# Weight buffers at three offsets within 128 bytes of SBUF, in a two-layer decoder kernel

## The chip, the cores and the metric

The kernel runs on one core of a Trainium2 chip. The metric is the device time of one execution in microseconds; each version is timed in several runs and the median is taken. A profile is one further execution with the hardware profiler on, which gives a start and a duration for every instruction.

The engines are TensorE (PE in the profile, with its weight loads shown apart as PEld), VectorE (DVE), ScalarE (ACT), GpSimd (POOL) and SyncE (SP), which here issues the DMAs. They run side by side and wait for one another through semaphores. SBUF is the on-chip memory with 128 partitions; a tile's address is an offset in bytes within each partition. PSUM takes the products of TensorE.

## What is computed

Two decoder layers on 256 tokens of width 2048. Layer 0 is a sliding-window attention with 32 query heads, 8 key and value heads and a learned sink per head; layer 1 is an RG-LRU recurrent block. Each is followed by a gated feed-forward block with a short causal convolution over positions. Cut to what matters here:

```python
def conv_ffn(h, w_up, conv_w, conv_b, w_down):
    u = causal_dwconv(h @ w_up, conv_w, conv_b)        # 2048 -> 2 x 6144, 3 taps
    g, v = jnp.split(u, 2, axis=-1)
    return (jax.nn.gelu(g, approximate=True) * v) @ w_down

for layer in range(2):
    h = rmsnorm(x, mix_norm[layer])
    x = x + (sliding_window_attention(h, ...) if layer == 0 else rglru_block(h, ...))
    x = x + conv_ffn(rmsnorm(x, ffn_norm[layer]), ...)
```

All inputs and the output are float32. The matrices hold some 100 million weights, each of which is read once.

## The kernel before

**Layout.** Activations stay in SBUF, transposed: features on partitions, the 256 tokens along the free axis. Weights come from HBM in chunks of 1 MiB, [128 partitions x 2048] float32, 376 of them in one fixed list (`order`): keys 4, values 4, queries 16, attention output 16, then the first feed-forward block with 96 up-projection and 48 down-projection chunks, recurrent input 32, recurrent output 16, and the second feed-forward block with 96 and 48 again. The gates of the recurrent block have 8 smaller loads of their own.

**Two parts of each weight.** A float32 weight `w` is split into `hi` and `lo`, two numbers in the shorter format float32r whose sum is `w`. Activations are split likewise. A product is hi*hi + hi*lo + lo*hi. With a block of 128 x 128 weights stationary, `hi` meets 512 columns, the activation's two parts side by side (`mm_hi`, line 183), and `lo` meets 256 columns, the activation's first part (`mm_lo`, line 189). A chunk holds 16 such blocks, so it makes 16 matmuls of 512 columns and then 16 of 256, each with its own weight load of 128 columns. In the down projections a chunk is used as two half batches of 8 and 8.

**The stream of chunks.** Each chunk passes three buffers: `raw` (written by a DMA that SyncE issues, line 102), `hi` (ACT casts `raw`, line 109) and `lo` (DVE subtracts `hi` from `raw`, line 117). Each of the three has its own pool with three buffers, which the chunks take in turn. `advance()` issues one DMA, one cast and one subtraction, for chunks ahead of the one in use; it is called after each chunk's matmuls. The order of instructions on every engine is the order in which the program is written.

**Moving operands.** The queries, keys, up projections (`pu`) and the recurrent input projection (`px`, `py`) stream `h`, which lies in the pool `per`. The attention's output projection (`po`) streams `ao`, the down projections (`pd`) `g`, the recurrent output projection (`pr`) `z`: these lie in pools that are opened after the weight pools, behind them in SBUF. In the value projection (`pv`) the roles are swapped: `h` is stationary and the weights stream.

**Where tiles lie.** A pool lays its tiles one behind another in the order in which they are first asked for; small tiles take at least 32 bytes. In `per` the tiles ahead of the weights have sizes of whole multiples of 128 bytes but for the last three, `sp`, `sp4` and `sp8`, of 64 bytes each. Every weight buffer has 8192 bytes, so all nine start at 64 modulo 128. `x` and `h` start at 0 modulo 128.

**Small attention tiles.** `kg` (two gains), `kq` (their product, one column), `snk` (the sinks) and `nsnk` (their negative), and `rc`, `rct`, `rcv` (two columns each, for the norm's factor along the partitions) are tiles of their own in the pool `attn`.

Of the kernel before, what the change touches and what calls it, by code (L numbers as in the profile page):

```python
"""Two decoder layers on one core: sliding-window attention with sinks + ConvFFN, then an RG-LRU
block + ConvFFN.

Activations stay on chip, transposed: features on partitions, the 256 tokens along the free
axis.  Weights stream through SBUF once, in 1 MiB chunks.  A float32 operand is split exactly into
two float32r parts (w = hi + lo, 12 significant bits each); a product is hi*hi + hi*lo + lo*hi,
accumulated in float32 in PSUM.  With the weight's part stationary, hi streams [x_hi | x_lo] and lo
streams x_hi, so a projection's PSUM bank holds hi*hi in its first half and the cross terms in its
second.

RMSNorm's per-token factor is applied to a projection's output, since it commutes with the product.
"""
# [7 lines left out]
F32 = mybir.dt.float32  # L20
F32R = mybir.dt.float32r
AF = mybir.ActivationFunctionType
ALU = mybir.AluOpType
# [17 lines left out]
def trunk(ctx, tc, xT, wq, wk, wv, wo, win, wg, wout, wup, wdn, mixg, ffng, kqg, sinks,  # L41
# [10 lines left out]
    hip = ctx.enter_context(tc.tile_pool(name="hip", bufs=3))  # L52
    lop = ctx.enter_context(tc.tile_pool(name="lop", bufs=3))
# [51 lines left out]
    def split_hi():  # L105
        c = st["hi"]
        if c < NCH:
            his[c] = hip.tile([P, CH], F32R, tag="hi", name=f"hi{c}")
            act.copy(out=his[c], in_=raws[c])  # L109
            st["hi"] += 1  # L110

    def split_lo(part=slice(0, CH)):
        c = st["lo"]
        if c < NCH:
            if part.start == 0:
                los[c] = lop.tile([P, CH], F32R, tag="lo", name=f"lo{c}")
            dve.tensor_tensor(out=los[c][:, part], in0=raws[c][:, part], in1=f(his[c][:, part]), op=ALU.subtract)  # L117
            if part.stop == CH:
                raws.pop(c)
                st["lo"] += 1  # L120
# [6 lines left out]
    def use():  # L127
        """The next chunk's parts."""
        c = st["use"]
        st["use"] += 1  # L130
        return his.pop(c), los.pop(c)
# [5 lines left out]
    def step(g):  # L137
        """Runs a generator to its next yield."""
        if g is not None:
            next(g, None)  # L140

# [1 line left out]
    def split_x(dst, src, gains, k):  # L143
        """dst[:, k] = the two parts of src * gain (src [P, T])."""
        act.activation(out=dst[:, k, 0, :], in_=src, func=AF.Copy, scale=gains[:, k:k + 1])
        dve.scalar_tensor_tensor(out=dst[:, k, 1, :], in0=src, scalar=gains[:, k:k + 1],
                                 in1=f(dst[:, k, 0, :]), op0=ALU.mult, op1=ALU.subtract)

    def stat(src, first):
        """sqa += src * src (src [P, 2, T])."""  # L150
        if first:
            pool.tensor_tensor(out=sqa, in0=src, in1=src, op=ALU.mult)
        else:
            pool.tensor_tensor(out=sqt, in0=src, in1=src, op=ALU.mult)  # L154
            pool.tensor_tensor(out=sqa, in0=sqa, in1=sqt, op=ALU.add)
# [5 lines left out]
    def rsqrt1(y, v):  # L161
        """A first guess of v ** -0.5."""
        act.activation(out=y, in_=v, func=AF.Ln)
        act.activation(out=y, in_=y, func=AF.Exp, scale=-0.5)

    def rsqrt2(y, v, tmp):
        """One Newton step towards v ** -0.5."""
        dve.tensor_tensor(out=tmp, in0=v, in1=y, op=ALU.mult)
        dve.scalar_tensor_tensor(out=tmp, in0=tmp, scalar=-0.5, in1=y, op0=ALU.mult, op1=ALU.mult)
        dve.scalar_tensor_tensor(out=y, in0=tmp, scalar=1.5, in1=y, op0=ALU.add, op1=ALU.mult)  # L170
# [21 lines left out]
    def x_epi(ps, d, n, gains, tp, out_=None, tag="xt"):  # L192
        """x's tiles d .. d + n take the product in ps [P, n, 512]; then h's, or the output's."""
        t = tp.tile([P, n, T], F32, tag=tag, name=f"xt{st['use']}")
        xs = x[:, d:d + n, :]
        for i in ([slice(0, n)] if out_ is None else [slice(i, i + 1) for i in range(n)]):
            dve.tensor_tensor(out=t[:, i], in0=ps[:, i, 0:T], in1=xs[:, i], op=ALU.add)  # L197
            dve.tensor_tensor(out=xs[:, i], in0=ps[:, i, T:], in1=t[:, i], op=ALU.add)  # L198
            if out_ is not None:
                nc.sync.dma_start(out=out_[:, d:d + n, :][:, i], in_=xs[:, i])  # L200
        if out_ is not None:
            return
        yield
        if gains is None:
            return
        for i in range(d, d + n):
            split_x(h, x[:, i, :], gains, i)
        yield
        if n == 2:
            stat(xs, d == 0)  # L210
        elif d % 2:
            stat(x[:, d - 1:d + 1, :], d == 1)

    def late_pair(ps, rhs, mid=None):
        """Two output tiles whose operand's last two k-tiles come late."""
        parts = [use(), use()]
        for i, (hi, lo) in enumerate(parts):
            mm_hi(ps[:, i], hi, rhs, rng(0, KD - 2))
            mm_lo(ps[:, i], lo, rhs, rng(0, KD - 2), stop=False)
        advance()  # L220
        if mid:
            mid()
        for i, (hi, lo) in enumerate(parts):
            mm_hi(ps[:, i], hi, rhs, rng(KD - 2, KD), start=False)
            mm_lo(ps[:, i], lo, rhs, rng(KD - 2, KD))
        advance()

    def softplus():
        """sp = softplus(-lam) = max(-lam, 0) + log1p(e), e = exp(-|lam|), by the series of
        log1p(e) = 2 artanh(z), z = e / (2 + e) <= 1/3."""  # L230
# [25 lines left out]
    for c in range(3):  # L256
        raws[c] = rawp.tile([P, CH], F32, tag="raw", name=f"raw{c}")
        his[c] = hip.tile([P, CH], F32R, tag="hi", name=f"hi{c}")
        los[c] = lop.tile([P, CH], F32R, tag="lo", name=f"lo{c}")
# [12 lines left out]
    # ================= attention =================  # L272
    with ExitStack() as ph:
# [10 lines left out]
        kq = ap_.tile([P, 1], F32, name="kq")  # L284
        kg = ap_.tile([P, 2], F32, name="kg")
        snk = ap_.tile([P, 32], F32, name="snk")
        nsnk = ap_.tile([P, 32], F32, name="nsnk")
        cb = ap_.tile([P, T], F32, name="cb")
        cc = ap_.tile([P, 2, 2], F32, name="cc")
        rc = ap_.tile([P, 2], F32, name="rc")  # L290
        rct = ap_.tile([P, 2], F32, name="rct")
        rcv = ap_.tile([P, 2], F32, name="rcv")
# [16 lines left out]
        # key j of two blocks is seen from query i when i < j <= i + 128  # L309
# [36 lines left out]
        dve.tensor_scalar(out=nsnk, in0=snk, scalar1=-1.0, scalar2=None, op0=ALU.mult)  # L346

# [13 lines left out]
        def k_fin(p):  # L361
# [11 lines left out]
            dve.scalar_tensor_tensor(out=s, in0=s, scalar=kq[:, 0:1], in1=r, op0=ALU.mult, op1=ALU.mult)  # L373
# [5 lines left out]
        def kv_norm():  # L379
            """The first norm's factor along the free axis and along the partitions."""  # L380
# [97 lines left out]
        def softmax(j, S):  # L478
            # column 2 * b + a: block b, head a
# [15 lines left out]
            ns = nsnk[:, 2 * j:2 * j + 2].unsqueeze(1).to_broadcast([P, 2, 2])  # L495
# [39 lines left out]
        def values(j):  # L535
# [3 lines left out]
            for b in range(2):  # L539
                # (key block, slice of the transposed probabilities)  # L540
# [15 lines left out]
        def attend(j, ps, hi, lo, rhs, nk):  # L556
            """One output tile's products over nk of its k-tiles; between them the steps of the
            attention of the query tiles j - 1 and j - 2."""
# [79 lines left out]
    # ================= ConvFFN =================  # L638
# [64 lines left out]
    # ================= RG-LRU =================  # L703
    with ExitStack() as ph:
# [6 lines left out]
        def projected(ps, n, eng):  # L711
            """A pair of output tiles: the two halves of the bank added, times the norm's factor."""
# [8 lines left out]
        with ExitStack() as px:  # L721
# [48 lines left out]
            def gates_rest(n, ps):  # L770
                """r (kept in a), i * x (in u), and t = tanh(4 sp r)."""
# [54 lines left out]
        # a = exp(-8 sp r) = 1 - t (1 + a), and sqrt(1 - a a) = sqrt(t) (1 + a)  # L826
# [37 lines left out]
        # (n, i): what follows the products of tile i of the y projection's pair n, before the stream  # L864
        # moves on and after it
# [58 lines left out]
def _layout(inp):  # L924
    import numpy as np

    def cols(w):
        """[K, N] -> [N / 128, 128, K / 128, 128]: chunk per 128 columns, rows on partitions."""
# [3 lines left out]
    def vec(v):  # L932
        """[..., n * 128] -> [128, ..., n]"""
# [49 lines left out]
```

## Time and profile before

| what | value |
|---|---|
| median of 3 runs | 2217.95 us (2217.54 to 2218.45) |
| span of the profiled execution | 2215.8 us |
| PE busy (matmuls) | 2185.9 us, 99% |
| PEld busy (weight loads) | 1921.5 us, 87% |
| DVE, ACT, POOL busy | 1568.6, 1142.7, 186.7 us |
| subtractions for `lo` (line 117) | 390 pieces, 858.1 us, 2200 ns each |
| casts for `hi` (line 109) | 373, 713.0 us, 1912 ns each |
| DMA | 405.15 MB, mean 183 GB/s |

The only execution time of the profiled run that the profile gives is its span, from the first to the last instruction; the median of the runs is 2.15 us above it. In the timeline view each row has a start, a duration, the engine, the line, the operation, the tile written and those read, shapes, and how many instructions are merged into it. A matmul's duration reaches past the start of the next one, since matmuls are pipelined; the rate is read from start to start.

### The profile page before, as it was taken

The page shows a single profiled execution, that of the slowest core. Times are in us where ns is not written, and L with a number is a line of the kernel's source. Part 1 is how long each engine was busy: PE and PEld are TensorE (multiplying, and loading weights), DVE is VectorE, ACT ScalarE, POOL GpSimd, SP SyncE. Part 2 cuts the span into 40 slices and gives each one's busy share as a digit, 9 for nine tenths or more (in the row PEclk, how much of TensorE's full clock was granted, in tenths as well). Part 3 has the DMA queues.
Part 4 walks back from the last instruction along what each step waited for, and adds up shares of the span by engine and source line. Part 5 has one row for each costly group of instructions (what it writes and reads, how often), then busy time and mean ns, then how long its engine had stood idle before and what let it go on. Part 6 is the DMA issues. An engine that isn't in the chain of part 4 may idle for free.

```text
span 2215.8 us, 30701 instructions
## 1 busy us (share of the span) xinstructions
PE 2185.9 (99%) x12656; PEld 1921.5 (87%) x12656; DVE 1568.6 (71%) x1862; ACT 1142.7 (52%) x1400; POOL 186.7 (8%) x155
## 2 busy tenths in 40 slices
PE   7999999999999999999999979999999999999999
PEld 6888888888888888888889868888888888888888
DVE  7877767777644777776677787777776457777654
ACT  4777445555433555553366744455554335555432
POOL 4122220000000000002200143200000000000000
PEclk9999999999999999999999999999999999999999
DMA  6333555555555555555465445555555555555543
GB/s 218 134 116 116 189 189 208 191 190 190 190 186 194 187 192 191 191 190 189 163 223 176 163 152 194 186 191 190 190 190 192 190 188 190 190 190 190 190 190 133
DMA packets 61053, 405.15 MB, mean 183 GB/s; under 512 B 7537, under 2 KB 9969, under 8 KB 13169
## 3 DMA queue, kind: packets, MB, share of 16 engines
q1 hardware_dynamic: 60912, 403.19, 51.3%
q8 instruction: 99, 1.62, 0.3%
q14 instruction: 42, 0.34, 0.0%
HBM read 401.06 MB, written 2.10 MB: 182 GB/s over the span
## 4 chain that ended last, share of the span: by engine, by line
PE 93%; DVE 3%; ACT 2%; issue 1%; POOL 1%; DMA 0%; SPq 0%; DVEq 0%; ACTq 0%
PE pu L183 32%; PE pu L189 16%; PE pd L183 16%; PE pd L189 8%; PE px L183 3%; PE po L183 3%; PE pr L183 3%; PE pq L183 2%; PE px L189 2%; PE pr L189 1%; PE po L189 1%; PE pq L189 1%; PE O L544 1%; DVE lo L117 1%; POOL ps L717 1%
## 5 line engine op out<-in xcount | busy, mean ns | idle before, releaser
L117 DVE TENSOR_TENSOR lo<-raw,hi 128x2048 fp32r<-128x2048 f32 (+1 forms) x390 | 858.1, 2200 | 223.8 <-ACT hi L109 222.6
L109 ACT CAST hi<-raw 128x2048 fp32r<-128x2048 f32 x373 | 713.0, 1912 | 386.1 <-PE pd L183 248.0
L183 PE MATMUL pu<-h,hi 128*128 128x512 f32 x3072 | 736.7, 392 | 0.0
L183 PEld LDWEIGHTS pu<-h,hi 128*128 128x128 f32 x3072 | 563.0, 188 | 111.2
L189 PEld LDWEIGHTS pu<-h,lo 128*128 128x128 f32 x3072 | 383.5, 188 | 16.4
L189 PE MATMUL pu<-h,lo 128*128 128x256 f32 x3072 | 387.0, 278 | 0.0
L183 PE MATMUL pd<-g,hi 128*128 128x512 f32 x1536 | 384.6, 392 | 0.0
L183 PEld LDWEIGHTS pd<-g,hi 128*128 128x128 f32 x1536 | 276.2, 189 | 49.4
L189 PEld LDWEIGHTS pd<-g,lo 128*128 128x128 f32 x1536 | 209.6, 190 | 14.9
L189 PE MATMUL pd<-g,lo 128*128 128x256 f32 x1536 | 214.2, 282 | 0.0
L666 ACT CAST g<-us 128x256 fp32r<-128x256 f32 x96 | 39.0, 406 | 280.7 <-DVE us L665 280.7
L659 DVE SCALAR_TENSOR_TENSOR uy<-us,fw,uy 128x255 f32<-128x255 f32 (+1 forms) x384 | 176.7, 481 | 6.8
L651 DVE TENSOR_TENSOR us<-pu,ua 128x512 f32<-128x512 f32 x96 | 66.4, 692 | 154.7 <-ACT ua L650 154.6
L650 ACT COPY ua<-pu 128x512 f32<-128x512 f32 x96 | 56.3, 587 | 143.4 <-PE pu L189 143.4
L656 ACT ACTIVATE uy<-us,fb,fw 128x256 f32<-128x256 f32 x192 | 104.8, 596 | 2.7 <-DVE us L652 2.7
L197 DVE TENSOR_TENSOR xt<-pd,x 128x512 f32<-128x512 f32 (+1 forms) x40 | 23.3, 583 | 83.3 <-PE pd L189 83.3
L154 POOL TENSOR_TENSOR sqt<-x 128x512 f32<-128x512 f32 x28 | 64.5, 2305 | 179.1 <-DVE x L198 176.6
L183 PE MATMUL px<-h,hi 128*128 128x512 f32 x320 | 77.7, 395 | 0.0
L667 DVE TENSOR_TENSOR g<-us,g 128x256 fp32r<-128x256 f32 x96 | 40.8, 425 | 45.3 <-ACT g L666 45.3
L183 PE MATMUL pr<-z,hi 128*128 128x512 f32 x256 | 63.1, 396 | 8.8 <-DVE z L861 7.8
L183 PE MATMUL pq<-h,hi 128*128 128x512 f32 x256 | 71.3, 403 | 0.2 <-DVE vh L442 0.2
L183 PEld LDWEIGHTS px<-h,hi 128*128 128x128 f32 x320 | 58.8, 189 | 11.8
(195 smaller groups left out, 1844.2 us busy)
## 6 DMA issues: line engine op xcount, KB each, us to landing
raw<-in_wup SPq DMA_DIRECT2D x192, 1024.0 KB, 4.8
raw<-in_wdn SPq DMA_DIRECT2D x96, 1024.0 KB, 4.8
raw<-in_win SPq DMA_DIRECT2D x32, 1024.0 KB, 4.8
raw<-in_wq SPq DMA_DIRECT2D x16, 1024.0 KB, 4.7
raw<-in_wo SPq DMA_DIRECT2D x16, 1024.0 KB, 4.8
raw<-in_wout SPq DMA_DIRECT2D x16, 1024.0 KB, 4.8
raw<-in_wv SPq DMA_DIRECT2D x4, 1024.0 KB, 5.4
graw<-in_wg SPq DMA_DIRECT2D x8, 512.0 KB, 3.4
```

The lines of the kernel that those rows point to most:

```text
L109: act.copy(out=his[c], in_=raws[c])
L117: dve.tensor_tensor(out=los[c][:, part], in0=raws[c][:, part], in1=f(his[c][:, part]), op=ALU.subtract)
L154: pool.tensor_tensor(out=sqt, in0=src, in1=src, op=ALU.mult)
L183: pe.matmul(ps, lhsT=hi[:, off + k * n:off + k * n + P], rhs=rhs[:, xk].rearrange("p a t -> p (a t)"), start=start and k == ks[0][0], stop ...
L189: pe.matmul(ps[:, T:], lhsT=lo[:, off + k * n:off + k * n + P], rhs=rhs[:, xk, 0, :], start=False, stop=stop and k == ks[-1][0])
L197: dve.tensor_tensor(out=t[:, i], in0=ps[:, i, 0:T], in1=xs[:, i], op=ALU.add)
L650: act.copy(out=a, in_=ps[:, :, 0:T])
L651: dve.tensor_tensor(out=s, in0=ps[:, :, T:], in1=a, op=ALU.add)
L656: act.activation(out=y[:, i, :], in_=s[:, i, :], func=AF.Identity, scale=fw[:, layer, n, 2:3], bias=fb[:, layer, n:n + 1])
L659: dve.scalar_tensor_tensor(out=y[:, i, tap:], in0=s[:, i, 0:T - tap], scalar=fw[:, layer, n, 2 - tap:3 - tap], in1=y[:, i, tap:], op0=ALU. ...
L666: act.copy(out=g[:, m, 0, :], in_=s[:, 0, :])
L667: dve.tensor_tensor(out=g[:, m, 1, :], in0=s[:, 0, :], in1=f(g[:, m, 0, :]), op=ALU.subtract)
```

## The change

The three `hi` buffers and the three `lo` buffers are no longer three buffers of one tag, but three tags of one buffer each, taken by the chunk's number modulo 3. Behind each is a pad of 64, 32 and 32 bytes that nobody uses, so that the three start at 64, 0 and 32 modulo 128. The pads of a pool sum to 128 bytes, so what follows starts at the same offset modulo 128 as before. `raw` stays as it was. Of the small attention tiles, `kq` becomes the first column of `kg`, `nsnk` is written over `snk`, and `rc`, `rct`, `rcv` become columns of one tile. Comments were removed, with line numbers kept.

```diff
-    hip = ctx.enter_context(tc.tile_pool(name="hip", bufs=3))
-    lop = ctx.enter_context(tc.tile_pool(name="lop", bufs=3))
+    hip = ctx.enter_context(tc.tile_pool(name="hip", bufs=1))
+    lop = ctx.enter_context(tc.tile_pool(name="lop", bufs=1))
...
+    def part_tile(c, pool_, what):
+
+        return pool_.tile([P, CH], F32R, tag=f"{what}{c % 3}", name=f"{what}{c}")
+
+    def pad(pool_, what, n):
+        pool_.tile([P, n // 4], F32, name=f"pad_{what}{n}_{len(pads)}")
+        pads.append(n)
+
+    pads = []
...
-            his[c] = hip.tile([P, CH], F32R, tag="hi", name=f"hi{c}")
+            his[c] = part_tile(c, hip, "hi")
             act.copy(out=his[c], in_=raws[c])
...
-                los[c] = lop.tile([P, CH], F32R, tag="lo", name=f"lo{c}")
+                los[c] = part_tile(c, lop, "lo")
...
     for c in range(3):
         raws[c] = rawp.tile([P, CH], F32, tag="raw", name=f"raw{c}")
-        his[c] = hip.tile([P, CH], F32R, tag="hi", name=f"hi{c}")
-        los[c] = lop.tile([P, CH], F32R, tag="lo", name=f"lo{c}")
+        his[c] = part_tile(c, hip, "hi")
+        pad(hip, "hi", (64, 32, 32)[c])
+        los[c] = part_tile(c, lop, "lo")
+        pad(lop, "lo", (64, 32, 32)[c])
...
-        kq = ap_.tile([P, 1], F32, name="kq")
         kg = ap_.tile([P, 2], F32, name="kg")
+        kq = kg[:, 0:1]
         snk = ap_.tile([P, 32], F32, name="snk")
-        nsnk = ap_.tile([P, 32], F32, name="nsnk")
...
-        rc = ap_.tile([P, 2], F32, name="rc")
-        rct = ap_.tile([P, 2], F32, name="rct")
-        rcv = ap_.tile([P, 2], F32, name="rcv")
+        rcs = ap_.tile([P, 3, 2], F32, name="rcs")
+        rc, rct, rcv = rcs[:, 0], rcs[:, 1], rcs[:, 2]
...
-        dve.tensor_scalar(out=nsnk, in0=snk, scalar1=-1.0, scalar2=None, op0=ALU.mult)
+        dve.tensor_scalar(out=snk, in0=snk, scalar1=-1.0, scalar2=None, op0=ALU.mult)
...
-            ns = nsnk[:, 2 * j:2 * j + 2].unsqueeze(1).to_broadcast([P, 2, 2])
+            ns = snk[:, 2 * j:2 * j + 2].unsqueeze(1).to_broadcast([P, 2, 2])
```

More of the change, by code (lines that the diff above doesn't have):

```diff
@@ L372, in k_fin @@
             rsqrt2(r, v, t)
-            dve.scalar_tensor_tensor(out=s, in0=s, scalar=kq[:, 0:1], in1=r, op0=ALU.mult, op1=ALU.mult)
+            dve.scalar_tensor_tensor(out=s, in0=s, scalar=kq, in1=r, op0=ALU.mult, op1=ALU.mult)
             for i in range(2):
```

## The prediction

> **What bounds the kernel now.** I read the page first, then stretches of single stages, then the order of TensorE's instructions in time.
>
> ```profile
> span 2215.8 us, 30701 instructions
> PE 2185.9 (99%) x12656; PEld 1921.5 (87%) x12656; DVE 1568.6 (71%) x1862; ACT 1142.7 (52%) x1400; POOL 186.7 (8%) x155
> PE 93%; DVE 3%; ACT 2%; issue 1%; POOL 1%; DMA 0%; SPq 0%; DVEq 0%; ACTq 0%
> ...
> L117 DVE TENSOR_TENSOR lo<-raw,hi 128x2048 fp32r<-128x2048 f32 (+1 forms) x390 | 858.1, 2200 | 223.8 <-ACT hi L109 222.6
> L109 ACT CAST hi<-raw 128x2048 fp32r<-128x2048 f32 x373 | 713.0, 1912 | 386.1 <-PE pd L183 248.0
> ```
>
> TensorE is never without work, and the chain that ended last is 93% TensorE. Two stretches, one of the up projection and one of the down projection (columns: length, then busy time and count for PE, PEld, DVE, ACT, POOL, then granted clock, DMA share, GB/s):
>
> ```profile
> 325.00:436.00 111.00, 111.00 (x646) 97.64 (x645) 87.50 (x105) 65.33 (x75) 0.00 (x0) 1.00 0.57 200
> 600.00:655.00 55.00, 55.00 (x318) 48.48 (x317) 26.71 (x16) 19.10 (x10) 0.00 (x0) 1.00 0.55 191
> ```
>
> No gap and a granted clock of 1.00. So the time is the number of matmuls times their pitch (start to start), and only a changed pitch moves the end. The pitch is not one number. In the order of time, TensorE's batches of `hi` (512 columns) and `lo` (256 columns), up projection, then output projection of the attention, then down projection:
>
> ```profile
> 325.16 3.84 PE L183 MATMUL pu<-h,hi 128*128 128x512 f32 x16
> 328.84 1.98 PE L189 MATMUL pu<-h,lo 128*128 128x256 f32 x16
> 330.65 3.82 PE L183 MATMUL pu<-h,hi 128*128 128x512 f32 x16
> 334.31 2.05 PE L189 MATMUL pu<-h,lo 128*128 128x256 f32 x16
> 336.20 1.09 PE L183 MATMUL pu<-h,hi 128*128 128x512 f32 x4
> ```
>
> ```profile
> 240.79 3.82 PE L183 MATMUL po<-ao,hi 128*128 128x512 f32 x16
> 244.44 2.08 PE L189 MATMUL po<-ao,lo 128*128 128x256 f32 x16
> 246.36 0.86 PE L183 MATMUL po<-ao,hi 128*128 128x512 f32 x3
> ...
> 600.36 1.12 PE L189 MATMUL pd<-g,lo 128*128 128x256 f32 x8
> 601.32 2.00 PE L183 MATMUL pd<-g,hi 128*128 128x512 f32 x8
> 603.16 1.11 PE L189 MATMUL pd<-g,lo 128*128 128x256 f32 x8
> 604.11 2.00 PE L183 MATMUL pd<-g,hi 128*128 128x512 f32 x8
> ```
>
> From start to start, `pu` takes 3.68 + 1.81 us for one chunk and 3.66 + 1.89 for the next, 11.04 for two: **5.52 us a chunk**, with two kinds of `lo` batch (113 and 118 ns a matmul). `po` takes 3.65 + 1.92: **5.57** (120 ns a `lo`). `pd` takes 0.96, 1.84, 0.95 for half batches: 2 x (1.84 + 0.955) = **5.59**. Shapes, engine and clock are the same; the moving operand differs. From the tile sizes in the code, `h` starts at 0 modulo 128 bytes, while `ao`, `g` and all nine weight buffers start at 64: `sp`, `sp4` and `sp8` are 64 bytes each and every other long-lived tile ahead of the weights is a multiple of 128. So weights less moving operand is 64 for `pu` and 0 for `po` and `pd`. `z` is at 64 too, and its row agrees (3.65 and 1.92). The attention's value product has weights `vh` at 64 against `pt` at 0 (behind the small attention tiles, which take 32 bytes or more each):
>
> ```profile
> 1334.41 3.82 PE L183 MATMUL pr<-z,hi 128*128 128x512 f32 x16
> 1338.06 2.08 PE L189 MATMUL pr<-z,lo 128*128 128x256 f32 x16
> 1339.98 0.40 PE L183 MATMUL pr<-z,hi 128*128 128x512 f32 x1
> ...
> 110.17 1.22 PE L544 MATMUL O<-pt,vh 128*128 128x256 f32 x9
> 111.22 0.63 PE L183 MATMUL pq<-h,hi 128*128 128x512 f32 x2
> ```
>
> 1.05 us for 9 is 117 ns: like `lo` at difference 64, not the 120 of difference 0. I take it that a matmul's stream and the weight load that runs under it (PEld, 87% busy) delay each other, by an amount that depends on this difference. A `hi` less a `lo` of `po` is (3.65 - 1.92) / 16 = 108 ns for 256 columns, so the columns alone would be 216 and 108 ns; the excess of 12 ns on both is what one weight load costs there.
>
> **The change, part by part.** The instructions stay: same casts, subtractions, matmuls, DMAs, in the same order. Three tags with one buffer each, chosen by chunk modulo 3, rotate as one tag with three did, so each cast waits for the same matmuls as now (the 248.0 us behind L109, off the chain). Merging `kq` into `kg`, `nsnk` into `snk`, and `rc`, `rct`, `rcv` into one tile joins operations that already follow one another; a wait between them would come once, before the query tiles, and is bounded by one microsecond. I put it at 0. What moves is the weights' start: 64, 0 or 32 for chunks 0, 1, 2 modulo 3, `hi` and `lo` alike. `g`, `ao`, `z` stay at 64, since the pads sum to 256 bytes.
>
> DVE and ACT now read and write `hi` and `lo` at other offsets than `raw` (64). If that slows them it is hidden: in the stretch 325 to 436, 20 chunks long, DVE is idle for 23.5 us and ACT for 45.7, so a subtraction may grow by 1.2 us on its 2.2 and a cast by 2.3 on its 1.9 before TensorE waits. Only beyond that would each further 0.1 us cost 192 x 0.1 = 19 us. Nothing in the rows suggests it.
>
> TensorE, by stage (chunks of 1 MiB: `pu` 192, `pd` 96, `po` and `pr` 32, `px` and `py` 32, attention 24):
>
> - *Chunks that go to a known difference.* A third of `pu` goes from 64 to 0: 64 x (5.57 - 5.52) = **+3.2 us**. A third of `pd` goes from 0 to 64. Taking halves of the `pu` batches, 2 x (1.835 + 0.925) = 5.52: 32 x (5.52 - 5.59) = **-2.2**. For `po` and `pr`, 10.7 x (5.52 - 5.57) = **-0.5**.
> - *`pu` chunks that stay at 64.* Half of their `lo` batches run at 1.81 today, and which kind comes depends on how the `hi` batch ahead ended. With neighbours at other differences the fast kind may be lost: 64 x 0.04 = +2.6 at worst, or come always: -2.6. I take half the loss, **+1.3**, as the slow kind is what follows any disturbance in `px`:
>
> ```profile
> 1137.97 3.90 PE L183 MATMUL px<-h,hi 128*128 128x512 f32 x16
> 1141.70 2.05 PE L189 MATMUL px<-h,lo 128*128 128x256 f32 x16
> 1143.59 3.83 PE L183 MATMUL px<-h,hi 128*128 128x512 f32 x16
> 1147.25 2.05 PE L189 MATMUL px<-h,lo 128*128 128x256 f32 x16
> 1149.14 0.29 PE L765 MATMUL g<-xc,ghi 128*128 128x256 f32 x1
> ```
>
> - *`px`, `py`.* 11.17 / 2 = 5.585 with the gates between, against 5.57 at difference 0: **0**; attention likewise (24 chunks, some 0.4 us either way).
> - *Chunks at difference 32 (`pu`) or -32 (`pd`, `po`, `pr`).* No row shows this. Bounds from the rows: the best batches seen, 3.65 + 1.81 = 5.46, and the worst, 3.73 + 1.92 = 5.65. I take the middle between the two known differences, 5.545, because 32 lies between them: 64 x 0.025 - 32 x 0.045 - 10.7 x 0.025 = 1.6 - 1.4 - 0.3 = **-0.1**. At the lower bound it is -3.8 - 4.2 - 1.2 - 1.3 = -10.5, at the upper +8.3 + 1.9 + 0.9 + 0.7 = +11.8 (the last term is `px` and `py`).
>
> Sum: 3.2 - 2.2 - 0.5 + 1.3 - 0.1 = +1.7 on the span of 2215.8, so 2217.5. The median of the runs is 2217.95, 2.15 above the span, which gives **2219.7 us**.
>
> A rule speaks against any effect. The Trainium skill (TensorE: Matmul & The Clock Gate, Step-by-step: what each phase is for) says that weight loads and the moving operand have separate read ports, so "Loading the next tile's weights doesn't steal SBUF read bandwidth from the running matmul." By it the sum would be 0 and the time 2218.0. The trace does not bear it out: 113, 118 and 120 ns for one shape at clock 1.00.
>
> **The rivals.**
>
> *Nothing depends on the offset* (the change doesn't do what it says): the differences between `pu` and `po` come from something else about `h`, its place below the weights for instance. Then 2218.0. Against it: `O`, both of whose operands lie above the weights, runs like `pu`; `pr`, `po` and `pd` agree with each other. For it: the two kinds of `lo` exist at one offset, so something besides the offset counts. By the rule just named this is the outcome.
>
> *Difference 32 keeps the two streams apart.* Then the best rows hold: 1.8 - 10.5 gives 2218.0 + 1.8 - 10.5 = 2209 (1.8 is the sum without the -0.1). Were the load fully hidden, a chunk would be 16 x 324 ns = 5.19 us: 64 x -0.33 - 32 x 0.40 - 21.4 x 0.39 = -42, or 2177. For it: the rates do vary with the offset. Against: no stage, with whatever tile, shows a stream without the excess.
>
> *Difference 32 is the worst of all* (the slower side). Place: the weight loads of buffer 2, some 118 chunks (64 + 32 + 10.7 + 10.7) of 32 loads, 3,776 loads. A load that starts in the middle of a 64-byte piece touches nine pieces of its 512 bytes where it touched eight, and meets the stream once more; and the loads of `h`'s stages lose the fast `lo`. At the worst rows: 1.8 + 11.8 = +13.6, or 2231.6. Each nanosecond a load is 3.8 us, so it decides, past 0.2%, from about 1 ns a load above the middle; were the 12 ns paid twice it would be +45, or 2263. For it: 64 and 0, the known cases, both start on a piece of 64 bytes, and nothing tells what lies between. Against: the excess is small against 108 ns in every row. The Trainium skill (SBUF — State Buffer, Door 1) gives lines of 16 bytes, by which 32 would be as good a start as 64; no run here shows the line's size.
>
> **How the numbers follow.** Forecast 0.40, no dependence 0.08, apart 0.22, worst 0.30: the slower side is above the faster because the known terms are already at +1.8. What can be told from no change is 0.2%, 4.4 us, so 2213.5 to 2222.4 is the same. Forecast and no dependence fall there but for 0.01 on each side: faster 0.23, same 0.46, slower 0.31. The range takes in both bounds, 2209 and 2231.6, and part of the tails beyond: 2203 to 2240. The forecast's own range is 2214 to 2225.
>
> **What would show it.** Every third `pu` chunk should show 3.65 + 1.92 like `po`, and every third `pd` half chunk should fall from 0.955 to 0.91 to 0.945 for `lo`; the chunk after, of buffer 2, gives the price of 32 directly. If `pu` chunks of all three buffers keep the present pattern, the offset is not the cause. If DVE or ACT slow beyond the slack above, gaps appear in PE with L117 or L109 as releaser. A gap-free PE whose batches leave 3.65 to 3.73 or 1.81 to 1.92 makes the prediction wrong in its largest unknown.

## The result: 1% slower

The changed kernel takes a median of 2241.32 us (2240.86 to 2241.78) against 2218.2 us before: a ratio of **1.0106, interval 1.0092 to 1.012**. The forecast was 2219.7 us. The page's first lines, after:

```profile
span 2239.1 us, 30701 instructions
PE 2209.9 (99%) x12656; PEld 1934.2 (86%) x12656; DVE 1571.0 (70%) x1862; ACT 1141.1 (51%) x1400; POOL 186.6 (8%) x155
...
L126 DVE TENSOR_TENSOR lo<-raw,hi 128x2048 fp32r<-128x2048 f32 (+1 forms) x390 | 857.9, 2200 | 225.4 <-ACT hi L118 223.8
L118 ACT CAST hi<-raw 128x2048 fp32r<-128x2048 f32 x373 | 711.2, 1907 | 395.2 <-PE pd L192 251.2
```

The number of instructions on each engine is the same. Subtractions still take 2200 ns and casts 1907 (1912 before), so the offsets did not slow the subtractions and casts. TensorE's busy time grew by 24 us, and the part of the span in which it is not busy stayed (29.9 us before, 29.2 after). In two stretches of single stages it has no gap (columns: length, then busy time and count for PE, PEld, DVE, ACT, POOL, then granted clock, DMA share, GB/s):

```profile
329.00:430.00 101.00, 101.00 (x577) 88.49 (x576) 78.28 (x94) 56.64 (x66) 0.00 (x0) 1.00 0.55 195
600.00:655.00 55.00, 55.00 (x317) 48.18 (x317) 26.40 (x16) 19.07 (x10) 0.00 (x0) 1.00 0.54 192
```

The clock is 1.00 as before. So the pitch changed. Three consecutive chunks of an up projection, then two half batches of `hi` and of `lo` of a down projection, in the order of time (starts in the first column):

```profile
348.68 3.89 PE L192 MATMUL pu<-h,hi 128*128 128x512 f32 x16
352.41 2.08 PE L198 MATMUL pu<-h,lo 128*128 128x256 f32 x16
354.33 3.90 PE L192 MATMUL pu<-h,hi 128*128 128x512 f32 x16
358.06 2.05 PE L198 MATMUL pu<-h,lo 128*128 128x256 f32 x16
359.95 3.82 PE L192 MATMUL pu<-h,hi 128*128 128x512 f32 x16
363.61 2.09 PE L198 MATMUL pu<-h,lo 128*128 128x256 f32 x16
365.53 0.40 PE L192 MATMUL pu<-h,hi 128*128 128x512 f32 x1
```

```profile
607.08 1.99 PE L192 MATMUL pd<-g,hi 128*128 128x512 f32 x8
608.90 1.13 PE L198 MATMUL pd<-g,lo 128*128 128x256 f32 x8
609.87 2.01 PE L192 MATMUL pd<-g,hi 128*128 128x512 f32 x8
611.71 1.12 PE L198 MATMUL pd<-g,lo 128*128 128x256 f32 x8
612.67 2.02 PE L192 MATMUL pd<-g,hi 128*128 128x512 f32 x8
```

The up projection's chunks of buffers 2, 0 and 1 take 3.73 + 1.92 = 5.65, 3.73 + 1.89 = 5.62 and 3.66 + 1.92 = 5.58 us, where before two took 11.04. The mean is 5.617, against 5.517 before: 192 x (5.617 - 5.517) = **+19 us of the 23**. A down-projection chunk shown takes 1.82 + 0.97 + 1.84 + 0.96 = 5.59; averaged over the matmuls' starts it is 5.605 against 5.587, so 96 chunks give +1.7. The rest is spread over the other 88 chunks. The surprise is buffer 0: its `hi` and its `lo` start at 64 modulo 128 as ever, and a chunk in them costs 0.10 us more.

### The profile page after: what moved, and what is told of

It reads as the page before. It is cut to its first block, busy times and chain, and to the rows that moved or that the text cites. A ratio compares the mean times of both kernels' runs of the same rounds, so it can differ in the third digit from the quotient of the medians.

```text
span 2239.1 us, 30701 instructions
## 1 busy us (share of the span) xinstructions
PE 2209.9 (99%) x12656; PEld 1934.2 (86%) x12656; DVE 1571.0 (70%) x1862; ACT 1141.1 (51%) x1400; POOL 186.6 (8%) x155
## 4 chain that ended last, share of the span: by engine, by line
PE 93%; DVE 3%; ACT 2%; issue 1%; POOL 1%; DMA 0%; SPq 0%; DVEq 0%; ACTq 0%
PE pu L192 32%; PE pu L198 16%; PE pd L192 16%; PE pd L198 8%; PE px L192 3%; PE po L192 3%; PE pr L192 3%; PE pq L192 2%; PE px L198 2%; PE pr L198 1%; PE po L198 1%; PE pq L198 1%; PE O L553 1%; DVE lo L126 1%; POOL ps L726 1%
## 5 line engine op out<-in xcount | busy, mean ns | idle before, releaser
L118 ACT CAST hi<-raw 128x2048 fp32r<-128x2048 f32 x373 | 711.2, 1907 | 395.2 <-PE pd L192 251.2
L192 PE MATMUL pu<-h,hi 128*128 128x512 f32 x3072 | 744.2, 395 | 0.0
L198 PEld LDWEIGHTS pu<-h,lo 128*128 128x128 f32 x3072 | 394.0, 189 | 17.3
L198 PE MATMUL pu<-h,lo 128*128 128x256 f32 x3072 | 398.2, 282 | 0.0
```

Source lines behind the costliest of these rows:

```text
L192: pe.matmul(ps, lhsT=hi[:, off + k * n:off + k * n + P], rhs=rhs[:, xk].rearrange("p a t -> p (a t)"), start=start and k == ks[0][0], stop ...
L198: pe.matmul(ps[:, T:], lhsT=lo[:, off + k * n:off + k * n + P], rhs=rhs[:, xk, 0, :], start=False, stop=stop and k == ks[-1][0])
```

## The experiments

Except for the second experiment, each is an edit of the changed kernel; the sweeps and the last kernels leave its pads out.

**Which part of the change?** First the tiles and tags without the pads:

```diff
         his[c] = part_tile(c, hip, "hi")
-        pad(hip, "hi", (64, 32, 32)[c])
         los[c] = part_tile(c, lop, "lo")
-        pad(lop, "lo", (64, 32, 32)[c])
```

> The changed kernel without its pads: small attention tiles merged, three tags of one buffer each, all weight buffers at 64 modulo 128 again. Offset theory (the pads alone did it): 2218 us, within 0.1% of before, and a pu chunk of 5.52 us. Rival (the merged tiles or the separate tags cost the time through a wait): about 2241 us, with pauses on TensorE.

Measured: 2217.48 us, ratio 0.9997 (0.9988 to 1.0007). Merged tiles and separate tags cost nothing; the pads are all of it.

**Absolute start or difference?** The kernel before, with everything 32 bytes later:

```diff
+    per.tile([P, 8], F32, name="pad32")
     x = per.tile([P, KD, T], F32, name="x")
```

> The kernel before with 32 unused bytes ahead of everything: each tile starts 32 bytes later, so weights are at 96, h at 32, g at 96 modulo 128 and all differences stay. Theory of the difference (weights less moving operand counts): 2218 us, pu 5.52, pd 5.59 us a chunk. Rival (a load that starts off a 64-byte boundary is itself slow, whatever streams): all chunks pay what the chunk at 32 pays now, pu 5.65 us, so 376 x 0.1 = some 35 to 50 us more, 2255 to 2268 us.

Measured: 2218.3 us, ratio 1.0001 (0.9991 to 1.001). Of its up projections, in order of time:

```profile
472.37 1.98 PE L190 MATMUL pu<-h,lo 128*128 128x256 f32 x16
474.19 3.82 PE L184 MATMUL pu<-h,hi 128*128 128x512 f32 x16
477.85 2.05 PE L190 MATMUL pu<-h,lo 128*128 128x256 f32 x16
479.73 2.46 PE L184 MATMUL pu<-h,hi 128*128 128x512 f32 x10
```

1.82, 3.66 and 1.88: the batches of before. Each load now starts 32 bytes off a multiple of 64 and is no slower. A shift of all tiles alike by 32 bytes changes nothing, so it is not the weights' start in itself that counts; what the pads changed is the distance between tiles.

**Is it the mixing?** All six buffers at 32 modulo 128 (a pad of 96 ahead, 32 behind):

```diff
+        if c == 0:
+            pad(hip, "hi", 96)
         his[c] = part_tile(c, hip, "hi")
-        pad(hip, "hi", (64, 32, 32)[c])
         los[c] = part_tile(c, lop, "lo")
-        pad(lop, "lo", (64, 32, 32)[c])
+        if c == 2:
+            pad(lop, "lo", 32)
```

> All six weight buffers at 32 modulo 128, raw at 64 and the moving operands where they were: h stages at difference 32, g, ao and z stages at 96. If a difference of 32 is dear by itself: pu 5.65 us in every chunk, 192 x 0.13 = +25 us from pu alone, 2243 us or more. If only the mixing of three differences is dear, pu comes near the present 5.52 and the time near 2218 us.

Measured: 2241.55 us, ratio 1.0108 (1.0093 to 1.0123).

```profile
471.45 3.89 PE L192 MATMUL pu<-h,hi 128*128 128x512 f32 x16
475.18 2.06 PE L198 MATMUL pu<-h,lo 128*128 128x256 f32 x16
477.07 3.89 PE L192 MATMUL pu<-h,hi 128*128 128x512 f32 x16
```

3.73 + 1.89 = 5.62 us in every chunk (5.627 over many). One difference, no mixing, the same loss: a difference of 32 costs that much by itself, though buffers 0 and 1 of the changed kernel are not explained by that.

**A first sweep, which showed a wrong assumption.** A kernel in which every part's buffer is 128 bytes longer and the start used within it changes every 12 chunks, by 8 bytes in `pu` and 16 in `pd` (`cb` shares space with `nt` to make room; each of the sweeps ran once, and only its trace is read):

```diff
-        return pool_.tile([P, CH], F32R, tag=f"{what}{c % 3}", name=f"{what}{c}")
+        t = pool_.tile([P, CH + 32], F32R, tag=f"{what}{c % 3}", name=f"{what}{c}")
+        o = start_of(c) // 4
+        return t[:, o:o + CH]
```

> Parts in buffers 128 bytes longer, of which a chunk uses 8192 bytes from a start that changes every 12 chunks: in the up projections the difference steps through 0, 8, 16 to 120 bytes, in the down projections through 0, 16 to 112; elsewhere it is as before. No total is forecast. Theory of the difference: the chunk's time is a function of it, 5.57 us at 0, 5.52 at 64, about 5.65 at 32 for pu, and pd follows the same curve. Rival (mixing): inside a block of 12 chunks with one start, the chunk at 32 comes down to 5.52. Rival (absolute start): pu and pd differ by 64 bytes in where their worst start lies.

Within one block of 12, where every chunk has the same start modulo 128, times still repeat by three, the buffers. Here is the block at difference 0:

```profile
330.62 3.82 PE L210 MATMUL pu<-h,hi 128*128 128x512 f32 x16
334.28 2.08 PE L216 MATMUL pu<-h,lo 128*128 128x256 f32 x16
336.20 3.81 PE L210 MATMUL pu<-h,hi 128*128 128x512 f32 x16
339.84 2.09 PE L216 MATMUL pu<-h,lo 128*128 128x256 f32 x16
341.77 3.89 PE L210 MATMUL pu<-h,hi 128*128 128x512 f32 x16
```

5.58 and 5.57 here, and 5.63 for the third, whose `hi` batch is the last row. Buffers 8320 bytes apart share their place modulo 128 but not modulo 256 or 512. So 128 was too short a period. It also gave a suspect for buffer 0: in the changed kernel the pads of `hi`'s pool move `lo` by 128 bytes against `hi`, and those of both move `g`, `ao` and `z` by 256.

**The sweep with buffers that agree modulo 512.** 512 bytes longer instead, steps of 32 in `pu` and 64 in `pd`; `cb`, `vt`, `nt` and two key tiles share space with others to make room.

> The sweep again with buffers 512 bytes longer, so that all six keep one place modulo 512: the common difference modulo 512 steps by 32 from -64 to 416 in the up projections (12 chunks each) and by 64 from 0 to 448 in the down projections; three small tiles share space to make room. If 512 bytes are the period, every block shows chunk times that no longer repeat by three (the buffers), -64 gives the 5.52 us of before, 0 gives 5.57 to 5.59 and 32 the 5.63 of the kernel with all buffers at 32, and pu and pd follow one curve. If the period is longer, the repeat by three stays. If 128 is the period, the curve repeats every 128.

The repeat by three is gone but for the block at 128, where chunks still differ by 0.02 us, and the layers agree: in all eight pairs of `pu` blocks whose differences are 256 apart the means are equal to 0.001 us. A chunk at -64 (first layer) and one at 192 (second layer):

```profile
335.76 3.84 PE L209 MATMUL pu<-h,hi 128*128 128x512 f32 x16
339.44 1.98 PE L215 MATMUL pu<-h,lo 128*128 128x256 f32 x16
341.25 1.07 PE L209 MATMUL pu<-h,hi 128*128 128x512 f32 x4
...
1447.64 3.84 PE L209 MATMUL pu<-h,hi 128*128 128x512 f32 x16
1451.32 1.98 PE L215 MATMUL pu<-h,lo 128*128 128x256 f32 x16
1453.13 3.82 PE L209 MATMUL pu<-h,hi 128*128 128x512 f32 x16
```

At -64 and 192 the chunk takes 3.68 + 1.81 (the faster of two kinds that take turns there, as before; the other is 3.66 + 1.88), at 160 and 416 every chunk after the first two takes 3.73 + 1.92. So the **period is 256 bytes**, not 512 as expected and not 128. From start to start, averaged over the last eight chunks of a block (us a chunk; `pd` was stepped by 64):

| weights less moving operand, modulo 256 | 0 | 32 | 64 | 96 | 128 | 160 | 192 | 224 |
|---|---|---|---|---|---|---|---|---|
| `pu` | 5.566 | 5.626 | 5.547 | 5.646 | 5.623 | 5.654 | **5.517** | 5.600 |
| `pd` | 5.586 | | 5.547 | | 5.620 | | **5.513** | |

The kernel before had its up projections at 192, the best place of the curve, and its down projections at 0. `pu` and `pd` follow one curve within 0.02 us, though DVE is busy for 73% of the `pu` block at 0 (36.40 of 50 us) and for 50% of the `pd` block at 0 (24.99 of 50): that speaks against the work of DVE and ACT beside the matmuls as the cause. The kernel with all buffers at 32 fits too: its down projections were at 224 by this count and took 5.600.

**Undoing one side of the change at a time.** First the same starts, with pads that sum to 512, so that `lo` keeps its place to `hi`, and `g` to both (`cb` and two key tiles share space to make room):

```diff
-        pad(hip, "hi", (64, 32, 32)[c])
+        pad(hip, "hi", (64, 32, 416)[c])
-        pad(lop, "lo", (64, 32, 32)[c])
+        pad(lop, "lo", (64, 32, 416)[c])
```

> The changed kernel with the third pad at 416 in place of 32 bytes, so that a pool's pads sum to 512: the starts are still 64, 0 and 32 modulo 128, but lo keeps its place to hi, and g to both, modulo 512. If only the place modulo 128 counts: as the changed kernel, 2241 us, buffer 0's pu chunk 5.62 us. If the place modulo 512 counts: buffer 0's pu chunk at 5.52 to 5.55, buffer 1's at 5.57, buffer 2's at 5.63, mean 5.57 to 5.58, some 2229 us.

Measured: 2226.77 us, ratio 1.004 (1.0025 to 1.0056). Buffers 2, 0 and 1 in turn:

```profile
464.61 3.89 PE L192 MATMUL pu<-h,hi 128*128 128x512 f32 x16
468.33 2.06 PE L198 MATMUL pu<-h,lo 128*128 128x256 f32 x16
470.23 3.84 PE L192 MATMUL pu<-h,hi 128*128 128x512 f32 x16
473.90 1.98 PE L198 MATMUL pu<-h,lo 128*128 128x256 f32 x16
475.71 3.82 PE L192 MATMUL pu<-h,hi 128*128 128x512 f32 x16
479.37 2.07 PE L198 MATMUL pu<-h,lo 128*128 128x256 f32 x16
481.28 2.02 PE L192 MATMUL pu<-h,hi 128*128 128x512 f32 x8
```

5.62, 5.48 and 5.57 us, near the curve's values at 32, 192 and 0 (5.626, 5.517 and 5.566); buffer 0 lies below its value because it has the fast kind of `lo` (1.81) each time. The three offsets as such cost 9 us, so 14.5 of the 23 are gone once `lo` keeps its place. Then the other side: pads all behind the buffers, so that every buffer is at 64 modulo 128 as before, and only `lo` and what lies behind have moved:

```diff
         his[c] = part_tile(c, hip, "hi")
-        pad(hip, "hi", (64, 32, 32)[c])
         los[c] = part_tile(c, lop, "lo")
-        pad(lop, "lo", (64, 32, 32)[c])
+        if c == 2:
+            pad(hip, "hi", 128)
+            pad(lop, "lo", 128)
```

> The changed kernel with each pool's 128 bytes of pad all behind its three buffers: every weight buffer starts at 64 modulo 128 as in the kernel before, but lo lies 128 bytes further from hi modulo 512, and the moving operands behind lie 256 bytes further. If only the place modulo 128 counts: 2218 us. If the place modulo 512 counts: pu chunks at the 5.62 us that buffer 0 has in the changed kernel, 192 x 0.10 = +20 us, about 2238 us.

Measured: 2238.89 us, ratio 1.0095 (1.0081 to 1.0108).

```profile
470.53 3.90 PE L192 MATMUL pu<-h,hi 128*128 128x512 f32 x16
474.26 2.04 PE L198 MATMUL pu<-h,lo 128*128 128x256 f32 x16
476.15 3.90 PE L192 MATMUL pu<-h,hi 128*128 128x512 f32 x16
```

3.73 + 1.89 = 5.62 in every chunk. **A pad that changes no buffer's offset within 128 bytes costs 21 us**, nearly what the whole change costs. Of the two moves in it, the 256 bytes of `g`, `ao` and `z` are a whole period, so what counts is the 128 bytes of `lo`. The two sides don't add (9 + 21 against 23), since each moves a chunk to a place of its own on the curve.

**`hi` and `lo` at differences of their own.** The sweep's buffers, with 16 pairs in the up projections and 8 in the down projections, 12 chunks each:

```diff
-        o = start_of(c) // 4
+        o = start_of(c, what) // 4
```

> As the sweep with steps of 32, but hi and lo start at differences of their own: in the up projections hi at 0 (first layer) or 192 (second), and lo at 0, 32 to 224 for 12 chunks each; in the down projections hi at 0 with lo at 64, 128, 192, 224, then hi at 192 with lo at 0, 64, 128, 160. If a batch of matmuls is set by the difference of the weights that load under it alone: hi batches take 3.65 us at 0 and 3.67 at 192 whatever lo does, lo batches 1.91 at 0, 1.82 at 64 and 1.81 to 1.88 at 192, so hi at 0 with lo at 64 gives 5.47 us a chunk, under the 5.52 of before. If the phase that one batch leaves decides the next (carry), the hi batches change with lo by up to 0.08 us.

Some of the pairs, with the pair 192, 64 in `pu` and then in `pd` as rows:

| `hi`, `lo` (modulo 256) | 0, 0 | 0, 64 | 0, 128 | 0, 224 | 192, 64 | 192, 128 | 192, 192 |
|---|---|---|---|---|---|---|---|
| `pu`, us a chunk | 5.567 | 5.540 | 5.567 | 5.527 | 5.620 | 5.567 | 5.517 |
| `pd` | | 5.560 | 5.614 | 5.560 | **5.493** | 5.600 | |

```profile
1583.36 3.90 PE L214 MATMUL pu<-h,hi 128*128 128x512 f32 x16
1587.10 2.04 PE L220 MATMUL pu<-h,lo 128*128 128x256 f32 x16
1588.98 3.19 PE L214 MATMUL pu<-h,hi 128*128 128x512 f32 x13
...
1781.08 2.00 PE L214 MATMUL pd<-g,hi 128*128 128x512 f32 x8
1782.92 1.07 PE L220 MATMUL pd<-g,lo 128*128 128x256 f32 x8
1783.83 0.39 PE L214 MATMUL pd<-g,hi 128*128 128x512 f32 x1
```

The simple picture fails: `lo` batches are fast where both parts are at 64 or at 192, but `hi` at 0 with `lo` at 64 gives 5.540, not 5.47, and one pair, 192 and 64, is 5.62 in `pu` and 5.493 in `pd`, where batches are half as long. The `hi` batch changes with `lo`'s place: `hi` at 192 takes 3.66 to 3.68 us with `lo` at 192, and 3.74 with `lo` at 64. So one batch leaves a state that the next starts from; what that state is, no run shows. The pair 192, 64 is what buffer 0 of the changed kernel has, and its 5.62 is the 5.62 seen there. The kernel with the pads behind has this pair in `pu` and 0, 128 in `pd`, and takes 5.62 and 5.61 there, against 5.620 and 5.614 in this sweep.

**Steps of 8 bytes.** The common difference once more, 6 chunks to a block.

```diff
-            return 32 * (8 * layer + 4 * half + k // 12)
-        return 64 * (4 * layer + 2 * half + (k - 48) // 12)
+            return (8 * (16 * layer + 8 * half + k // 6) + 64) % 256
+        return 16 * (8 * layer + 4 * half + (k - 48) // 6)
```

> The common difference again, in steps of 8 bytes from 0 to 248 in the up projections and of 16 bytes in the down projections, 6 chunks each. Places that the coarse sweep had must come back: 5.57 us at 0, 5.63 at 32, 5.55 at 64, 5.65 at 96, 5.52 at 192. If the chip sees 64-byte pieces, the places between behave like their neighbours at 32; if it sees 16-byte lines, steps of 8 give pairs of equal values and new values between.

The earlier places came back within 0.01 us: 5.56 at 0, 5.63 at 32, 5.55 at 64, 5.65 at 96, 5.52 at 192. Between them the curve is rough: 5.54 at 8, 5.62 at 16, 5.62 at 248, 5.58 at 200. Neither pieces of 64 bytes nor lines of 16 come out as plateaus. All 32 places in `pu` lie between 5.517 and 5.653, and 192 is the lowest.

**A kernel that uses it.** If 192 is the best place, the streams that are at 0 should go there. The weights stay where the kernel before has them; 64 unused bytes ahead of `ao`, `g` and `z` move the moving operands:

```diff
+        ap_.tile([P, 16], F32, name="aopad")
         ao = ap_.tile([P, KD, 2, T], F32R, name="ao")
...
+            gp.tile([P, 16], F32, name=f"gpad{layer}")
             g = gp.tile([P, KH, 2, T], F32R, name=f"g{layer}")
...
+        zp.tile([P, 16], F32, name="zpad")
         z = zp.tile([P, KD, 2, T], F32R, name="z")
```

> All weights at 64 as in the kernel before; g, ao and z start 64 bytes later, so that the down, output and recurrent output projections have the difference -64 that the up projections have today. If the difference alone decides: pd falls from 5.59 to 5.52 us a chunk and po and pr from 5.57 to 5.52, 96 x 0.07 + 28 x 0.05 = 8 us less, 2210 us. If the rate belongs to the stage (its half batches, its tile) and not to the difference: 2218 us.

Measured: 2208.97 us, ratio 0.996 (0.9948 to 0.9972).

```profile
654.65 2.00 PE L192 MATMUL pd<-g,hi 128*128 128x512 f32 x8
656.49 1.07 PE L198 MATMUL pd<-g,lo 128*128 128x256 f32 x8
657.39 1.99 PE L192 MATMUL pd<-g,hi 128*128 128x512 f32 x8
659.22 1.11 PE L198 MATMUL pd<-g,lo 128*128 128x256 f32 x8
660.16 2.00 PE L192 MATMUL pd<-g,hi 128*128 128x512 f32 x8
```

1.84 + 0.90 + 1.83 + 0.94 = 5.51 us a chunk, from 5.59, with no change to the place of `raw`, `hi` and `lo`, so their places to one another, which ACT and DVE work on, are not what decides. Last, the better pair for half batches, by `lo` buffers 256 bytes longer, of which the down projections' chunks use the part from byte 128 on (`cb` shares space with `nt` again):

```diff
+        t = pool_.tile([P, CH + 64], F32R, tag=f"{what}{c % 3}", name=f"{what}{c}")
+        k = c - 40 if c < 184 else c - 232
+        o = 32 if 0 <= k < 144 and k % 72 >= 48 else 0
+        return t[:, o:o + CH]
```

> The kernel with g, ao and z 64 bytes later, and in the down projections alone lo starts another 128 bytes later, so that hi is at 192 and lo at 64 modulo 256 there; all other stages have 192 for both. By the sweep of hi and lo a pd chunk takes 5.493 us in place of 5.513: 96 x 0.02 = 1.9 us under the kernel with only the move, some 2207 us. If the gain in the sweep came from the neighbours in its blocks, 2209 us.

> The kernel with g, ao and z 64 bytes later once more, beside the one above on the same chip: 2209 us, 9 us under the kernel before.

Measured on one chip: 2206.53 us, ratio 0.9948 (0.9934 to 0.9962), and 2208.74 us, 0.9958 (0.9945 to 0.9971), for the move alone. The intervals of the two overlap; the medians differ by the 2 us expected, each of the five runs of the first (2206.25 to 2206.87) lies below each of the second (2207.51 to 2209.52), and a `pd` chunk takes 5.496 us against 5.515. The first is the fastest kernel here.

## Why the prediction was wrong, point by point

- *What bounds the kernel* was right: TensorE, 99% busy, time as count times pitch, and nothing lost on DVE or ACT. ("Never without work" is too strong: it is not busy for some 30 us of the span, before and after alike.) The reading that the pitch depends on weights less moving operand was right too: moving everything changes nothing (2218.3), moving either side alone does (2241.55, 2208.97).
- *The step that failed first* is "64, 0 or 32 for chunks 0, 1, 2 modulo 3, `hi` and `lo` alike". It took places modulo 128, because only 0 and 64 were to be seen. The period is 256, and modulo 256 the pads of `hi`'s pool move `lo` by 128 bytes against `hi`. Less `h`, the pairs of `hi` and `lo` went from 192 and 192 to 192 and 64, 0 and 128, and 32 and 160 for the three buffers. With `lo` kept in its place the same three starts cost 9 us, so this step is worth 14.5 of the 23. The term "`pu` chunks that stay at 64", put at +1.3 us, was 64 x 0.103 = +6.6. "`g`, `ao`, `z` stay at 64" did hold: the 256 bytes by which they moved are a whole period.
- *Chunks that go to a known difference.* For `pu`, 5.58 against the 5.57 put down. That is luck: the pair there is 0 and 128, not 0 and 0, and the two happen to cost the same (5.567 each). For `pd` the -2.2 us did not come: the chunks of buffer 1 went from 5.59 to 5.60, not to 5.52. Modulo 128 their new place looked like that of the up projections; modulo 256 it is 64 and 192, where the up projections of before have 192 for both. The gain from 0 to the place of the up projections is real, 5.59 to 5.51, and came in the kernel that moved `g`.
- *The unseen difference of 32* was the second step, a term sized wrongly. It was put at the middle, 5.545. It measured 5.626 for a common difference and 5.65 for buffer 2 (the pair 32 and 160), the upper bound of 5.65: 64 x 0.133 = +8.5 us in place of +1.6. Two known points of a curve said nothing about the third.
- *The rivals.* "Nothing depends on the offset" is refuted by the trace: 5.52 to 5.65 us for the same work at the same clock. The Trainium skill (TensorE: Matmul & The Clock Gate, Step-by-step: what each phase is for) says that loading the next weights takes no read bandwidth from the running matmul; the 5.52 to 5.65 us do not agree with it if the load is what delays the stream. "32 keeps the two streams apart" is refuted by the 5.626. (Its fully hidden chunk, 16 x 324 ns, is 5.18 and not 5.19 us, which changes nothing else.) "32 is the worst" had the sign, and a far end of 2263; its reason, nine pieces of 64 bytes in place of eight, is refuted by the kernel with everything 32 bytes later. Nor was 32 the worst: 160 is, at 5.654.
- *The range* ended at 2240, 1 us under the result. The unseen chunks came in about where their upper bound put them (`pu` +8.5 against +8.3), and with that bound the working gave 2231.6; the other 10 us are chunks whose difference was taken as known, and whose price had no bound or too low a one (+2.6 at worst for `pu` in buffer 0, against +6.6).

What stays open is why the curve has its shape. The pitch depends on the distance of weights and moving operand modulo 256 and on what the batch before leaves; which parts of the chip meet there, no run here shows. That the weight load under the moving stream is its partner is argued from the dependence on the two starts, not tried by leaving loads out.

## What to carry to other kernels

Where TensorE is the bound and the trace has no gaps, read the pitch from start to start, stage by stage: differing pitches for one shape at one clock may be a loss that moving a tile recovers (9 us here). A pad may not be neutral: it also moves what lies behind it, so hold every other pair of operands where it was, or state what has moved, before a time is put down to an offset. Sweep the distance inside one kernel, a few chunks to each value, rather than guess between two points.

## What was not expected of the hardware

The time of a float32r matmul stream with a weight load for each matmul depends on the distance of the two operands in SBUF modulo 256 bytes, from 5.517 to 5.654 us for 16 matmuls of 512 and 16 of 256 columns (2.5%), and steps of 8 bytes still change it. The pattern is regular: after a block's first chunks, a chunk's time returns to within 0.01 us at most distances, and at 192 two kinds, 5.49 and 5.55 us, take turns.
